# Own buffers and an earlier load for two row chunks of an up projection, and a decode order squeezed by three half features

## The chip, the cores and the metric

The kernel runs on one core of a Trainium2 chip. The metric is the device time of one execution in microseconds (us), the median of three runs. TensorE (PE) multiplies matrices, VectorE (DVE), ScalarE (ACT) and GpSimd (POOL) work on rows of 128 partitions, SyncE (SP) issues most of the DMAs. Every engine has one instruction stream of its own, which it works through in order.

## The reference

One layer step of a hybrid decoder: a 2048-token prompt and eight sample tokens that attend to 4096 cached positions in pages. All arithmetic is float32. The part that matters here is the gated convolutional feed-forward network of the prompt rows, and the paged attention of the samples, which the kernel works on during it:

```python
def conv_ffn(h, prefix, w_up, conv_w, conv_b, w_down):
    up = h @ w_up                                  # h 2064 x 1024, w_up 1024 x 5632
    ...
    c = conv_b + sum(conv_w[i] * ext[:, i:i + L] for i in range(CONV_W))   # CONV_W = 3
    gate, val = c[..., :D_FF], c[..., D_FF:]       # D_FF = 2816 = 22 x 128
    out = (jax.nn.silu(gate) * val) @ w_down
```

For the samples, keys and values (8 heads of 64) are read through `page_table`; the weights come from `sigmoid(q.k)` and a running product of `1 - sigmoid` over later positions.

## The kernel before

Three parts follow each other on PE: the projections, attention and output projection of the prompt, to about 1163 us; the **up projection**, from 1184 to 2263 us; and the **down projection** to the end.

**Up projection.** The normalised rows `h2_s` (in device memory) are cut into four chunks of 512 rows. A chunk's rows are loaded, transposed on PE (tile `tp3c` or `tp0`, four 128x128 transposes into one PSUM buffer) and split into a high part (a cast on ACT, L163) and a low part (a subtraction on DVE, L164); both stand in `h2c[ch]`. Only three chunks have room: chunk 0 in pool `pha`, chunks 1 and 2 in `phb`, and chunk 3 takes chunk 0's place. The main loop runs over 44 features `it`: 0 to 21 take the 22 gate and value blocks of the weights for chunks 0 and 1, 22 to 43 the same blocks for chunks 2 and 3. A feature holds two chunks `k`, each a **pair** of **groups** `s` (gate and value); a group is 24 matmuls (`mm3`: 8 blocks of 128 rows, three products of high and low parts) into one PSUM buffer `psu`. So there are 88 pairs (called steps below) and 176 groups, numbered from 0. Per group, ACT scales the result into `cv` (L976), DVE adds the two convolution taps (L979) and, except for chunk 0, the tile's edge from `carry` (L982, L984), and then copies the last two columns into `carry` (L986). That copy is the last reader of the group's PSUM buffer. The pool `psm` has six such buffers, used in turn by `psu` and by the transposes `tp3c`. The next feature's weights `uwr` are loaded by SP (L703) and split by ACT and DVE (`uwh`, `uwl`).

**Chunks 2 and 3** go through `h2_chunk(ch)`, called at feature 4 for chunk 2 and behind feature 21 for chunk 3. It makes two loads of 256 rows (1 MB, L766) into buffers of the tag `kvd`, and per load 16 transposes (L773) and four splits.

**Decode.** The `kvd` buffers (`KVB` = 4, 1 MB each) are otherwise for the gathers of cached keys and values (`gather`, L813, an indirect DMA that POOL issues; 128 of them). Keys are multiplied and summed on DVE (L826, L828), values multiplied on PE (tile `dav`, L896), all in a written order of 101 items: keys, weights, values, and last the sums. `DSTEP(i)` is the number of items that stand ahead of step i; an item, once placed, calls the gather of a tile three further on. At the last feature (`it` = 43) the remaining items are placed, the decode pool is closed, and the first activations and weights of the down projection are loaded (`act_first`, `wd_first`).

The scheduler orders each engine's stream from the program order and the dependences, so the place of a call in the source doesn't fix its place on an engine.

Of the kernel before, what the change touches and what calls it, by code (L numbers as in the profile page):

```python
# [8 lines left out]
F32 = mybir.dt.float32  # L9
F32R = mybir.dt.float32r  # L10
# [8 lines left out]
P = 128  # L19
D = 1024  # L20
NK = D // P
# [9 lines left out]
NF = DFF // P  # L31
# [6 lines left out]
TILES = [(0, NS + META)] + [(NS + META + P * i, P) for i in range(SEQ // P)]  # L38
# [5 lines left out]
HKB, KFB, CHB = 11, 4, 2  # L44
RAWB = 4
FSTEP = lambda i: 3 * i // 2
DSTEP = lambda i: 101 * i // 85
CW = 512
NCH = SEQ // CW
NSB = NS + 4  # L50
# [4 lines left out]
def f32(ap):  # L55
    return ap.bitcast(F32)
# [3 lines left out]
def hymba_kernel(  # L60
# [7 lines left out]
    nc = tc.nc  # L68
# [24 lines left out]
    h2_s = dram.tile([ACOLS, D], F32, name="h2_s")  # L93
# [6 lines left out]
    ident = con.tile([P, P], F32, name="ident")  # L100
# [61 lines left out]
    def split(hi, lo, src):  # L162
        nc.scalar.copy(hi, src)  # L163
        nc.vector.tensor_tensor(out=lo, in0=src, in1=f32(hi), op=ALU.subtract)  # L164
# [12 lines left out]
    psm = main.enter_context(tc.tile_pool(name="ps_mm", bufs=2, space=PSUM, reuse_waits="tile"))  # L177
# [520 lines left out]
    pha = h2ctx.enter_context(tc.tile_pool(name="h2a", bufs=1, reuse_waits="tile"))  # L698
    h2c = {}

    def load_up(f):
        wr = puw.tile([P, NK, P], F32, name="uwr")
        nc.sync.dma_start(out=wr, in_=w_up[:, f * P:(f + 1) * P].rearrange("(c p) f -> p c f", p=P))  # L703
        wh = puw.tile([P, NK, P], F32R, name="uwh")
        wl = puw.tile([P, NK, P], F32R, name="uwl")
        split(wh, wl, wr)
        return wh, wl

    def load_down(f, pool):
        wr = puw.tile([P, NK, P], F32, name="uwr").rearrange("p c n -> p (c n)")  # L710
        nc.sync.dma_start(out=wr, in_=w_down[f * P:(f + 1) * P, :])
        if pool is puw:
            wh = puw.tile([P, NK, P], F32R, name="uwh").rearrange("p c n -> p (c n)")
            wl = puw.tile([P, NK, P], F32R, name="uwl").rearrange("p c n -> p (c n)")
        else:
            wt = pool.tile([P, 2, D], F32R, name="wd")
            wh, wl = wt[:, 0, :], wt[:, 1, :]
        split(wh, wl, wr)
        return wh, wl, wr
# [4 lines left out]
    psm = ctx.enter_context(tc.tile_pool(name="pu_mm", bufs=6, space=PSUM, reuse_waits="tile"))  # L724
    HF = NF // 2

    def load_act(pool, hf, a0, n):
        ar = pool.tile([P, HF, P], F32, name="ar", bufs=1)
        nc.sync.dma_start(out=ar[:, :, :n], in_=act_s[hf * HF:(hf + 1) * HF, :, a0:a0 + n].rearrange("f p n -> p f n"))
        ah = pool.tile([P, HF, P], F32R, name="ah", bufs=1)  # L730
        al = pool.tile([P, HF, P], F32R, name="al", bufs=1)
        split(ah[:, :, :n], al[:, :, :n], ar[:, :, :n])
        return ah, al

    with ExitStack() as es:
        phb = es.enter_context(tc.tile_pool(name="h2b", bufs=2, reuse_waits="tile"))
# [20 lines left out]
        dec = es.enter_context(ExitStack())  # L757
        dp = dec.enter_context(tc.tile_pool(name="dec", bufs=KVB, reuse_waits="tile"))

        def h2_chunk(ch):  # L760

            h2c[ch] = (pha if ch == 3 else phb).tile([P, 2, NK, CW], F32R, name="h2c")
            for a2 in range(0, 4, 2):
                c0 = TILES[1 + 4 * ch + a2][0]
                xn2 = dp.tile([P, 4, 512], F32, name="xn3", tag="kvd").rearrange("p k f -> p (k f)")
                nc.sync.dma_start(out=xn2.rearrange("p (a d) -> p a d", a=2),  # L766
                                  in_=h2_s[c0:c0 + 2 * P, :].rearrange("(a p) d -> p a d", p=P))
                for a in (a2, a2 + 1):
                    xn = xn2[:, (a - a2) * D:(a - a2 + 1) * D]
                    for c4 in range(0, NK, 4):  # L770
                        tp = psm.tile([P, 4, P], F32, name="tp3c", tag="psu")
                        for c in range(4):
                            nc.tensor.transpose(tp[:, c, :], xn[:, (c4 + c) * P:(c4 + c + 1) * P], ident)  # L773
                        split(h2c[ch][:, 0, c4:c4 + 4, a * P:(a + 1) * P], h2c[ch][:, 1, c4:c4 + 4, a * P:(a + 1) * P], tp)

        def sample_conv():
            sc_v = state_conv.rearrange("b j f -> (b j) f")
# [20 lines left out]
        for b in range(NB):  # L798
            nc.sync.dma_start(out=pt4[:, b:b + 1],
                              in_=page_table[b, :].rearrange("(n o) -> n o", o=1).unsqueeze(1).broadcast_to([NPAGE, 4, 1]))  # L800
# [8 lines left out]
        def gather(t):  # L809

            b, j = divmod(t % 64, 8)
            kvt[t] = dp.tile([P, 4, 512], F32, name="kvd", tag="kvd")
            nc.gpsimd.indirect_dma_start(out=kvt[t].rearrange("p k f -> p (k f)"), out_offset=None,  # L813
                                         in_=ckr if t < 64 else cvr,
                                         in_offset=bass.IndirectOffsetOnAxis(ap=idx[:, b, j:j + 1], axis=0))
# [115 lines left out]
        tiles = []  # L931
        for t in order:
            tiles += [t] if not isinstance(t, tuple) else [t[1], t[1] + 1] if t[0] == "v" else []
        ahead = KVB - 1
        done = [0, ahead]
        for t in tiles[:ahead]:
            gather(t)

        def decode_to(n):
            while done[0] < min(n, len(order)):  # L940
                t = order[done[0]]
                done[0] += 1
                kind, t = t if isinstance(t, tuple) else ("k", t)
                {"k": decode_keys, "v": decode_values, "w": decode_weights}.get(kind, lambda t: decode_sums())(t)
                for _ in range({"k": 1, "v": 2}.get(kind, 0)):
                    if done[1] < 128:
                        gather(tiles[done[1]])
                        done[1] += 1

        ws_next = ws_first  # L950
        for it in range(2 * NF):
            half, f = divmod(it, NF)
            ws = ws_next
            if it + 1 < 2 * NF:
                ws_next = [load_up((it + 1) % NF), load_up(NF + (it + 1) % NF)]
            else:
                decode_to(len(order))
                dec.close()
                pdx = ctx.enter_context(tc.tile_pool(name="pdx", bufs=1, side="right", reuse_waits="tile"))
                act_first = load_act(pdx, 0, 0, P)  # L960
                wd_first = [load_down(c, puw) for c in range(3)]
            if it == 4:
                h2_chunk(2)
            if it == 12:
                sample_conv()
            for k in (2 * half, 2 * half + 1):
                with tc.issue_after(last_dve):
                    decode_to(DSTEP(2 * it + k % 2))
                cv = []
                for s in range(2):  # L970
                    fi = f + s * NF
                    ps = psm.tile([P, CW], F32, name="psu")
                    w = ws[s]
                    mm3(ps, [(w[0][:, c, :], w[1][:, c, :], h2c[k][:, 0, c, :], h2c[k][:, 1, c, :]) for c in range(NK)])
                    t = pu.tile([P, CW], F32, name=f"cv{s}")
                    nc.scalar.activation(out=t, in_=ps, func=AF.Identity, scale=cpar(2, fi), bias=cpar(3, fi))  # L976
                    for d in (1, 0):
                        o = 2 - d
                        nc.vector.scalar_tensor_tensor(out=t[:, o:], in0=ps[:, 0:CW - o], scalar=cpar(d, fi),  # L979
                                                       in1=t[:, o:], op0=ALU.mult, op1=ALU.add)  # L980
                    if k:
                        nc.vector.scalar_tensor_tensor(out=t[:, 0:1], in0=carry[:, 1:2, fi], scalar=cpar(1, fi),  # L982
                                                       in1=t[:, 0:1], op0=ALU.mult, op1=ALU.add)
                        nc.vector.scalar_tensor_tensor(out=t[:, 0:2], in0=carry[:, :, fi], scalar=cpar(0, fi),  # L984
                                                       in1=t[:, 0:2], op0=ALU.mult, op1=ALU.add)
                    last_dve = nc.vector.tensor_copy(carry[:, :, fi], ps[:, CW - 2:CW]).ins  # L986
                    cv.append(t)
                sg = pu.tile([P, CW], F32, name="sg")
                nc.scalar.activation(out=sg, in_=cv[0], func=AF.Sigmoid)
                nc.gpsimd.tensor_tensor(out=cv[1], in0=cv[0], in1=cv[1], op=ALU.mult)  # L990
                nc.gpsimd.tensor_tensor(out=sg, in0=sg, in1=cv[1], op=ALU.mult)
                nc.sync.dma_start(out=act_s[f, :, CW * k:CW * (k + 1)], in_=sg)
            if it == NF - 1:
                h2_chunk(3)

    h2ctx.close()

# [1 line left out]
    with ExitStack() as es:  # L999
# [129 lines left out]
        for hf in range(2):  # L1129
            wd = []  # L1130
            for c in range(HF):
                f = hf * HF + c
# [49 lines left out]
```

## Time and profile before

| | us |
|---|---|
| median of three runs | 2816.26 (2814.99 to 2817.17) |
| the profiled execution | 2817.6, its span 2815.9 |
| PE busy | 2699.1 (96% of the span) |
| DVE busy | 1800.5 (64%) |
| ACT busy | 1041.7 (37%) |
| POOL busy | 837.1 (30%) |

The span is the time from the first to the last instruction that the profiler saw; the rest of the execution's time, 1.7 us, lies around it. Shares are means over the three parts, which differ much.

### The profile page before, as it was taken

How to read it: one execution, taken by the hardware profiler on the slowest of the kernel's cores; microseconds unless marked ns; L12 is line 12 of the kernel's file. 1: busy time of each engine (PE TensorE's matmuls, PEld its weight loads, DVE VectorE, ACT ScalarE, POOL GpSimd, SP SyncE). 2: the span in 40 equal slices, each digit the busy share in tenths (PEclk: the TensorE clock that was granted, in tenths of full speed). 3: DMA queues.
4: the chain of work that ended last, by engine and by line, in shares of the span. 5: the costliest groups of instructions: out<-in, count | busy, mean ns of one | idle time of the engine just before them, and what ended most of it. 6: DMA issues, size and time to landing. Idle time of an engine off the chain costs nothing.

```text
span 2815.9 us, 39585 instructions
## 1 busy us (share of the span) xinstructions
PE 2699.1 (96%) x14623; PEld 2102.5 (75%) x14623; DVE 1800.5 (64%) x2989; ACT 1041.7 (37%) x1817; POOL 837.1 (30%) x995
## 2 busy tenths in 40 slices
PE   5899999999998999897999999999999999999998
PEld 4677777777776887686877777777777767777777
DVE  4587668867678578687977676777765441214434
ACT  4466557656565356422222223222222220002111
POOL 0132233332224023154555544445543200000000
PEclk9899999999998999998999999999999999999999
DMA  7642542454435432554565656546565584666551
GB/s 257 235 160 101 169 171 96 136 203 154 159 95 167 145 103 95 183 186 159 179 224 199 221 187 229 189 176 222 205 218 181 181 298 157 193 204 225 182 176 63
DMA packets 321190, 498.77 MB, mean 177 GB/s; under 512 B 24279, under 2 KB 229351, under 8 KB 304597
## 3 DMA queue, kind: packets, MB, share of 16 engines
q1 hardware_dynamic: 302565, 362.02, 39.1%
q0 software_dynamic: 18432, 134.23, 12.6%
q8 instruction: 115, 1.88, 0.3%
q14 instruction: 78, 0.64, 0.1%
HBM read 395.99 MB, written 100.59 MB: 176 GB/s over the span
## 4 chain that ended last, share of the span: by engine, by line
PE 84%; DVE 6%; DMA 4%; issue 3%; ACT 2%; POOL 1%; SPq 0%; POOLq 0%; DVEq 0%; ACTq 0%
PE psu L169 11%; PE psu L170 11%; PE psu L171 11%; PE psd L169 6%; PE psd L171 6%; PE psd L170 6%; PE po L569 5%; PE psm L169 4%; PE psm L170 4%; PE z L509 4%; PE psm L171 4%; PE tt L554 3%; DVE om L517 2%; PE dav L896 2%; PE pso L171 2%
## 5 line engine op out<-in xcount | busy, mean ns | idle before, releaser
L169 PE MATMUL psu<-h2c,uwh 128*128 128x512 f32 x1408 | 553.9, 393 | 0.0
L170 PE MATMUL psu<-h2c,uwh 128*128 128x512 f32 x1408 | 551.6, 392 | 0.0
L171 PE MATMUL psu<-h2c,uwl 128*128 128x512 f32 x1408 | 550.1, 391 | 0.0
L517 DVE TENSOR_TENSOR_SCAN om<-om,zero 128x513 f32<-128x513 f32 (+5 forms) x360 | 380.5, 1064 | 106.6 <-ACT om L510 58.9
L979 DVE SCALAR_TENSOR_TENSOR cv<-psu,par,cv 128x511 f32<-128x511 f32 x352 | 261.5, 743 | 162.6 <-ACT cv L976 161.0
L522 POOL TENSOR_TENSOR be<-be,om 128x512 f32<-128x512 f32 (+3 forms) x176 | 189.2, 1075 | 582.7 <-DVE om L517 364.3
L990 POOL TENSOR_TENSOR cv<-cv,cv 128x512 f32<-128x512 f32 x88 | 226.3, 2572 | 386.3 <-DVE cv L984 306.9
L169 PEld LDWEIGHTS psu<-h2c,uwh 128*128 128x128 f32 x1408 | 265.2, 188 | 79.0 <-issue 16.9
L170 PEld LDWEIGHTS psu<-h2c,uwh 128*128 128x128 f32 x1408 | 265.0, 188 | 64.0 <-issue 10.6
L171 PEld LDWEIGHTS psu<-h2c,uwl 128*128 128x128 f32 x1408 | 265.0, 188 | 59.7 <-issue 4.8
L510 ACT ACTIVATE om<-z,nbias 128x512 f32<-128x512 f32 (+5 forms) x360 | 213.6, 595 | 178.7 <-PE z L509 117.4
L976 ACT ACTIVATE cv<-psu,par 128x512 f32<-128x512 f32 x176 | 136.5, 776 | 249.9 <-PE psu L171 249.9
L1149 DVE TENSOR_TENSOR xt<-psd,xt 128x512 f32<-128x512 f32 x64 | 44.1, 691 | 286.4 <-PE psd L171 281.5
L511 ACT ACTIVATE be<-z,bias 128x512 f32<-128x512 f32 (+5 forms) x360 | 212.1, 592 | 2.3 <-DVE bm L527 1.2
L170 PE MATMUL psm<-hk,wh 128*128 128x512 f32 x512 | 208.5, 408 | 3.3 <-DVE hk L218 3.2
L169 PE MATMUL psm<-hk,wh 128*128 128x512 f32 x512 | 206.1, 408 | 3.1 <-ACT hk L217 2.6
L171 PE MATMUL psm<-hk,wl 128*128 128x512 f32 x512 | 206.1, 403 | 1.1 <-DVE wl L164 1.1
L163 ACT CAST uwh<-uwr 128x1024 fp32r<-128x1024 f32 x94 | 98.8, 1055 | 286.7 <-PE psu L170 278.2
L170 PE MATMUL psd<-wd,ah 128*128 128x512 f32 x512 | 200.7, 393 | 3.0 <-DVE wd L164 3.0
L169 PE MATMUL psd<-wd,ah 128*128 128x512 f32 x512 | 202.3, 398 | 0.0
L164 DVE TENSOR_TENSOR uwl<-uwr,uwh 128x1024 fp32r<-128x1024 f32 x94 | 121.3, 1293 | 125.2 <-ACT uwh L163 122.8
L171 PE MATMUL psd<-wd,al 128*128 128x512 f32 x512 | 201.1, 394 | 0.0
(240 smaller groups left out, 4816.7 us busy)
## 6 DMA issues: line engine op xcount, KB each, us to landing
hk<-hs_s SPq DMA_DIRECT2D x96, 512.0 KB
uwr<-in_w_up_dram SPq DMA_DIRECT2D x88, 512.0 KB
act_s<-sg SPq DMA_DIRECT2D x88, 256.0 KB
ar<-act_s SPq DMA_DIRECT2D x32, 704.0 KB
raw<-in_w_up_dram SPq DMA_DIRECT2D x40, 512.0 KB
xt<-in_x_prompt_dram SPq DMA_DIRECT2D x32, 512.0 KB
hs_s<-hk SPq DMA_DIRECT2D x32, 512.0 KB
uwr<-in_w_down_dram SPq DMA_DIRECT2D x22, 512.0 KB
```

Of the source, the lines that this page charges most:

```text
L164: nc.vector.tensor_tensor(out=lo, in0=src, in1=f32(hi), op=ALU.subtract)
L169: nc.tensor.matmul(ps, ah, bh, start=i == 0, stop=False)
L170: nc.tensor.matmul(ps, ah, bl, start=False, stop=False)
L171: nc.tensor.matmul(ps, al, bh, start=False, stop=i == n - 1)
L510: nc.scalar.activation(out=om[:M, e, 0:n], in_=z[:M, :n], func=AF.Sigmoid, scale=-SCALE, bias=nbias[:M, h:h + 1])
L511: nc.scalar.activation(out=be[:M, e, 0:n], in_=z[:M, :n], func=AF.Sigmoid, scale=SCALE, bias=bias[:M, h:h + 1])
L517: nc.vector.tensor_tensor_scan(out=rv, data0=rv, data1=zero[:M, 0:1].broadcast_to([M, n + 1]), initial=1.0 if top else st["prev"][:M, e, 0 ...
L522: (nc.gpsimd if cnt["mul"] % 2 == 0 else nc.vector).tensor_tensor(out=be[:M, e, m0:n], in0=be[:M, e, m0:n], in1=om[:M, e, m0 + 1:n + 1], o ...
L569: mm = nc.tensor.matmul(o, v_, a_, start=top and i < (2 if groups else 1), stop=low and i == len(prods) - 1, skip_group_check=True)
L976: nc.scalar.activation(out=t, in_=ps, func=AF.Identity, scale=cpar(2, fi), bias=cpar(3, fi))
L979: nc.vector.scalar_tensor_tensor(out=t[:, o:], in0=ps[:, 0:CW - o], scalar=cpar(d, fi), in1=t[:, o:], op0=ALU.mult, op1=ALU.add)
L990: nc.gpsimd.tensor_tensor(out=cv[1], in0=cv[0], in1=cv[1], op=ALU.mult)
```

## The change

Chunks 2 and 3 get a tag of their own, `xn3`, with two buffers of 128 rows (512 KB each). `h2_load` loads one tile of 128 rows, `h2_turn` transposes and splits it, and for a chunk's first two tiles loads the tile two further on behind it. The loads of tiles 0 and 1 stand one feature ahead of the turn. Chunk 2 is turned in two halves, at features 4 and 5; chunk 3 whole, behind feature 21. The gathers that are made ahead are called at step 2, the decode items run from step 4 to step 84, and the pool is closed and `act_first` loaded at feature 42.

```diff
-DSTEP = lambda i: 101 * i // 85
+DSTEP = lambda i: 101 * max(i - 3, 0) // 81
...
-        def h2_chunk(ch):
-            h2c[ch] = (pha if ch == 3 else phb).tile([P, 2, NK, CW], F32R, name="h2c")
-            for a2 in range(0, 4, 2):
-                c0 = TILES[1 + 4 * ch + a2][0]
-                xn2 = dp.tile([P, 4, 512], F32, name="xn3", tag="kvd").rearrange("p k f -> p (k f)")
-                nc.sync.dma_start(out=xn2.rearrange("p (a d) -> p a d", a=2), ...
+        h2x = {}
+        def h2_load(ch, a):
+            h2x[ch, a] = dp.tile([P, D], F32, name="xn3", bufs=2)
+            nc.sync.dma_start(out=h2x[ch, a], in_=h2_s[TILES[1 + 4 * ch + a][0]:TILES[1 + 4 * ch + a][0] + P, :])
+        def h2_turn(ch, a):
+            if a == 0:
+                h2c[ch] = (pha if ch == 3 else phb).tile([P, 2, NK, CW], F32R, name="h2c")
+            xn = h2x.pop((ch, a))
+            for c4 in range(0, NK, 4):
...
+                split(h2c[ch][:, 0, c4:c4 + 4, a * P:(a + 1) * P], h2c[ch][:, 1, c4:c4 + 4, a * P:(a + 1) * P], tp)
+            if a < 2:
+                h2_load(ch, a + 2)
...
-            else:
+            if it == 2 * NF - 2:
                 decode_to(len(order))
                 dec.close()
...
                 act_first = load_act(pdx, 0, 0, P)
+            if it == 2 * NF - 1:
                 wd_first = [load_down(c, puw) for c in range(3)]
-            if it == 4:
-                h2_chunk(2)
+            for ch, t0 in ((2, 4), (3, NF)):
+                if it == t0 - 1:
+                    h2_load(ch, 0)
+                    h2_load(ch, 1)
+            if it in (4, 5):
+                h2_turn(2, 2 * it - 8)
+                h2_turn(2, 2 * it - 7)
...
             for k in (2 * half, 2 * half + 1):
+                if 2 * it + k % 2 == 2:
+                    for t in tiles[:ahead]:
+                        gather(t)
...
             if it == NF - 1:
-                h2_chunk(3)
+                for a in range(4):
+                    h2_turn(3, a)
```

What becomes of this on the engines is shown at three places. On SP, around the start of the up projection and through features 0 to 5 (`pt` is the page table, `qb` a sample's query), before:

```order
L744 DMA xn_13105<-h_s 128x1024
L703 DMA uwr<-in_w_up_dram 128x8x128
L799 DMA pt_13128<-in_page_table_dram 128x1x1 x8
L819 DMA qb<-qd_s 128x512 x2
...
L703 DMA uwr<-in_w_up_dram 128x8x128
L766 DMA xn_13811<-h_s 128x2x1024
L703 DMA uwr<-in_w_up_dram 128x8x128
L992 DMA act_s<-sg 128x512
L766 DMA xn_13841<-h_s 128x2x1024
```

and now:

```order
L803 DMA pt_13128<-in_page_table_dram 128x1x1 x8
L823 DMA qb<-qd_s 128x512
L765 DMA xn_13638<-h_s 128x1024
L765 DMA xn_13640<-h_s 128x1024
L823 DMA qb<-qd_s 128x512
...
L703 DMA uwr<-in_w_up_dram 128x8x128
L765 DMA xn_13811<-h_s 128x1024
L765 DMA xn_13827<-h_s 128x1024
L703 DMA uwr<-in_w_up_dram 128x8x128
...
L765 DMA xn_16707<-h_s 128x1024
L765 DMA xn_16709<-h_s 128x1024
```

The loads of chunk 2's tiles 0 and 1 moved up to right behind the page table, four features ahead of their turn; those of tiles 2 and 3 stand behind the first half's turn, and chunk 3's first two behind the second half's.

On PE at chunk 3 (behind feature 21), before:

```order
L171 MATMUL psu<-h2c,uwl 128x512
L896 MATMUL dav<-kvd,zdec 32x512 x4
L773 MATMUL tp3c<-ident,xn_16872 128x128 x16
L773 MATMUL tp3c<-ident,xn_16902 128x128 x16
L169 MATMUL psu<-h2c,uwh 128x512
```

and now:

```order
L171 MATMUL psu<-h2c,uwl 128x512
L775 MATMUL tp3c<-ident,xn_16707 128x128 x8
L775 MATMUL tp3c<-ident,xn_16709 128x128 x8
L900 MATMUL dav<-kvd,zdec 32x512 x8
L775 MATMUL tp3c<-ident,xn_16876 128x128 x8
L775 MATMUL tp3c<-ident,xn_16892 128x128 x8
L169 MATMUL psu<-h2c,uwh 128x512
```

At chunk 2, where PE had the same 16 and 16 transposes in one place (ahead of group 16), it now has 8 and 8 there and 8 and 8 ahead of group 20.

On DVE, at the second of these half turns (`cv_13864`, `cv_13894`, `cv_13933` and `cv_13965` are groups 16 to 19; each carry copy frees the PSUM buffer of the group before it), now:

```order
L164 TENSOR_TENSOR h2c<-tp3c,h2c 128x4x128 x2
L996 COPY carry<-psu 128x2
L830 TENSOR_TENSOR kvd<-kvd,qb 128x2048 x2
L989 SCALAR_TENSOR_TENSOR cv_13864<-psu,par,cv_13864 128x511
L832 TENSOR_REDUCE zdec<-kvd 128x4x8 x2
L989 SCALAR_TENSOR_TENSOR cv_13864<-psu,par,cv_13864 128x510
L996 COPY carry<-psu 128x2
L989 SCALAR_TENSOR_TENSOR cv_13894<-psu,par,cv_13894 128x511
L989 SCALAR_TENSOR_TENSOR cv_13894<-psu,par,cv_13894 128x510
L996 COPY carry<-psu 128x2
L830 TENSOR_TENSOR kvd<-kvd,qb 128x2048
L164 TENSOR_TENSOR uwl<-uwr,uwh 128x1024
```

followed by

```order
L989 SCALAR_TENSOR_TENSOR cv_13933<-psu,par,cv_13933 128x511
L992 SCALAR_TENSOR_TENSOR cv_13933<-carry,par,cv_13933 128x1
L832 TENSOR_REDUCE zdec<-kvd 128x4x8
L989 SCALAR_TENSOR_TENSOR cv_13933<-psu,par,cv_13933 128x510
L994 SCALAR_TENSOR_TENSOR cv_13933<-carry,par,cv_13933 128x2
L164 TENSOR_TENSOR uwl<-uwr,uwh 128x1024
L989 SCALAR_TENSOR_TENSOR cv_13965<-psu,par,cv_13965 128x511
L992 SCALAR_TENSOR_TENSOR cv_13965<-carry,par,cv_13965 128x1
L164 TENSOR_TENSOR h2c<-tp3c,h2c 128x4x128 x3
L996 COPY carry<-psu 128x2
```

Before, all eight `h2c` subtractions of chunk 2 stood in one place, behind the copies of groups 14 and 15 and ahead of group 16's taps. Now three of the second half's stand ahead of the copy of group 18 (the last row), which stands behind the first part of group 19.

On POOL the first four gathers stand where they stood, behind the setup of the decode; the fifth, which stood behind the first pair's product, stands behind the third's, and the later ones follow three pairs later than before at first, in step at the end.

## Rows read from the trace of the kernel before

**Rows 1.** The page: busy time and its share of the span, and the share of each engine in the chain that ended last.

```profile
PE 2699.1 (96%) x14623; PEld 2102.5 (75%) x14623; DVE 1800.5 (64%) x2989; ACT 1041.7 (37%) x1817; POOL 837.1 (30%) x995
...
PE 84%; DVE 6%; DMA 4%; issue 3%; ACT 2%; POOL 1%; SPq 0%; POOLq 0%; DVEq 0%; ACTq 0%
```

**Rows 2.** Stretches of the up projection and after: its length, then busy time and instructions of PE, PEld, DVE, ACT and POOL, the granted TensorE clock (1.00 is the higher of its two levels), the DMA share and GB/s.

```profile
1207.00:1272.00 65.00, 65.00 (x288) 53.81 (x288) 55.86 (x63) 18.34 (x24) 36.80 (x18) 1.00 0.51 181
1272.00:1295.00 23.00, 8.39 (x38) 7.49 (x37) 15.97 (x22) 6.79 (x11) 6.92 (x5) 0.67 0.62 210
1295.00:1715.00 420.00, 420.00 (x1936) 329.36 (x1935) 311.81 (x412) 111.15 (x145) 211.57 (x127) 1.00 0.55 193
1720.00:1731.00 11.00, 7.49 (x46) 6.07 (x45) 8.97 (x14) 6.11 (x10) 5.49 (x4) 0.84 0.92 322
...
2263.00:2311.00 48.00, 40.99 (x170) 28.00 (x169) 25.43 (x40) 15.90 (x16) 2.57 (x2) 0.89 0.85 296
```

**Rows 3.** What PE waited for between 1207 and 2315 us: waiting instruction, what released it, us in total, times, longest.

```profile
PE tp3c L773 <- DMA xn<-h_s: 16.0, 3, 9.7
PE psd L169 <- ACT ah L163: 3.6, 1, 3.6
...
PE tp3c L773 <- DVE h2c L164: 2.1, 1, 2.1
```

**Rows 4.** PE's timeline at chunk 2: start, duration, instruction, and in brackets the idle time before it and what ended it.

```profile
1272.34 0.39 PE L171 MATMUL psu<-h2c,uwl 128*128 128x512 f32 x1
1282.41 3.64 PE L773 MATMUL tp3c<-ident,xn 128*128 128x128 f32 x16 [9.69 <-DMA xn<-h_s]
1290.98 3.65 PE L773 MATMUL tp3c<-ident,xn 128*128 128x128 f32 x16 [4.93 <-DMA xn<-h_s]
1294.28 0.78 PE L169 MATMUL psu<-h2c,uwh 128*128 128x512 f32 x1
...
1296.86 0.40 PE L169 MATMUL psu<-h2c,uwh 128*128 128x512 f32 x1
```

**Rows 5.** SP's timeline there: when the loads of chunk 2 were issued.

```profile
1275.45 0.37 SPq L766 DMA_DIRECT2D xn<-h_s  x1
...
1286.09 0.36 SPq L766 DMA_DIRECT2D xn<-h_s  x1
```

**Rows 6.** DVE's timeline there; a row with no bracket started with nothing idle before it, so that the step from one start to the next is what an instruction costs in a row of them.

```profile
1273.14 2.27 DVE L828 TENSOR_REDUCE zdec<-kvd 128x32 f32<-128x2048 f32 x1
1275.34 0.73 DVE L979 SCALAR_TENSOR_TENSOR cv<-psu,par,cv 128x510 f32<-128x510 f32 x1
1276.00 0.20 DVE L984 SCALAR_TENSOR_TENSOR cv<-carry,par,cv 128x2 f32<-128x2 f32 x1
1276.12 1.21 DVE L164 TENSOR_TENSOR uwl<-uwr,uwh 128x1024 fp32r<-128x1024 f32 x1
1277.26 0.74 DVE L979 SCALAR_TENSOR_TENSOR cv<-psu,par,cv 128x511 f32<-128x511 f32 x1
...
1279.09 2.28 DVE L826 TENSOR_TENSOR kvd<-kvd,qb 128x2048 f32<-128x2048 f32 x1
...
1286.95 1.88 DVE L164 TENSOR_TENSOR h2c<-tp3c,h2c 128x512 fp32r<-128x512 f32 x3
```

**Rows 7.** PE's timeline at chunk 3.

```profile
1719.95 0.39 PE L171 MATMUL psu<-h2c,uwl 128*128 128x512 f32 x1
1720.27 1.13 PE L896 MATMUL dav<-kvd,zdec 128*32 128x512 f32 x8
1722.76 1.94 PE L773 MATMUL tp3c<-ident,xn 128*128 128x128 f32 x16 [1.36 <-DMA xn<-h_s]
1726.84 3.56 PE L773 MATMUL tp3c<-ident,xn 128*128 128x128 f32 x16 [2.15 <-DVE h2c L164]
1730.14 0.49 PE L169 MATMUL psu<-h2c,uwh 128*128 128x512 f32 x1
```

**Rows 8.** SP's timeline there.

```profile
1716.13 0.82 SPq L766 DMA_DIRECT2D xn<-h_s  x1
...
1721.46 0.36 SPq L766 DMA_DIRECT2D xn<-h_s  x1
```

**Rows 9.** The chain that ended last, at the start of the up projection (the load of one 512 KB tile of rows, from issue to landing).

```profile
1175.88 5.98 DMA xn<-h_s
```

**Rows 10.** The chain that ended last, at the end of the up projection, and SP's timeline there.

```profile
2264.22 7.62 DMA ar<-act_s
2271.91 10.13 DMA raw<-wf_s
...
2236.69 0.37 SPq L729 DMA_DIRECT2D ar<-act_s  x1
```

**Rows 11.** Gathers of values late in the up projection: POOL's issues, the products on PE that use them (eight records are one gathered tile), and the spread of times from issue to landing of the last 13.

```profile
2160.36 0.99 POOL L813 DMA_INDIRECT kvd<-in_cache_v_dram,idx  x1 [0.16 <-issue]
2165.12 0.98 POOL L813 DMA_INDIRECT kvd<-in_cache_v_dram,idx  x1 [2.45 <-PE dav L896]
...
2168.74 1.13 PE L896 MATMUL dav<-kvd,zdec 128*32 128x512 f32 x8
2174.10 1.13 PE L896 MATMUL dav<-kvd,zdec 128*32 128x512 f32 x8
...
DMA to landing us min/median/max: 5.2/7.5/9.9
```

More of the change, by code (lines that the diff above doesn't have):

```diff
@@ L758, in hymba_kernel @@
         dp = dec.enter_context(tc.tile_pool(name="dec", bufs=KVB, reuse_waits="tile"))
-        def h2_chunk(ch):
-            h2c[ch] = (pha if ch == 3 else phb).tile([P, 2, NK, CW], F32R, name="h2c")
-            for a2 in range(0, 4, 2):
-                c0 = TILES[1 + 4 * ch + a2][0]
-                xn2 = dp.tile([P, 4, 512], F32, name="xn3", tag="kvd").rearrange("p k f -> p (k f)")
[L766 to L774, printed above, removed]
+        h2x = {}
[7 more added lines that the diff above has]
+            for c4 in range(0, NK, 4):
+                tp = psm.tile([P, 4, P], F32, name="tp3c", tag="psu")
+                for c in range(4):
+                    nc.tensor.transpose(tp[:, c, :], xn[:, (c4 + c) * P:(c4 + c + 1) * P], ident)
+                split(h2c[ch][:, 0, c4:c4 + 4, a * P:(a + 1) * P], h2c[ch][:, 1, c4:c4 + 4, a * P:(a + 1) * P], tp)
+            if a < 2:
+                h2_load(ch, a + 2)
         def sample_conv():
@@ L935, in hymba_kernel @@
         done = [0, ahead]
-        for t in tiles[:ahead]:
-            gather(t)
         def decode_to(n):
```

## The prediction

> **What bounds the kernel now.** First the page: PE is busy 96% of the span and holds 84% of the chain that ended last, DVE 64% and 6% [rows 1]. So time is won only where PE stands still or runs at its lower clock. Second, the stretches of the up projection: in most of it PE has no gap at all, 420.00 us busy of 420.00 at a granted clock of 1.00, and the same in the twelve groups ahead of chunk 2, 288 matmuls in 65.00 us, 5.42 us a group [rows 2]. There are three exceptions: 1272 to 1295 us, where PE is busy 8.39 us of 23.00 at 0.67; 1720 to 1731, 7.49 of 11.00; and the passage to the down projection from 2263, 40.99 of 48.00 [rows 2]. Third, the waits name the causes: 16.0 us are transposes waiting for loads of chunk rows, 2.1 us a transpose waiting for DVE, and the passage waits for something else, the activations' split [rows 3]. The reader is to see that the idle time of these stretches, 14.6, 3.5 and 7.0 us, is all there is, and that the change touches the first two.
>
> **Chunk 2, the large term.** The last matmul of group 15 starts at 1272.34; the next could start 0.23 later, and the next group's does at 1294.28: 21.7 us lost. That group's first six matmuls then take 2.58 us (1294.28 to 1296.86) where six at the full rate take 1.36: 1.2 us more for the clock. Together 22.9 us [rows 4]. The 9.69 and 4.93 us of idle time in it are the loads: the first is issued at 1275.45, right after the key reduction of 1273.14 that frees a shared buffer, and the second at 1286.09, behind the first 16 transposes [rows 4, 5, 6]. Now the first two tiles are loaded at the start of the up projection into buffers that nothing else uses, some 85 us before their turn; the other two are issued when the first half's transposes are done and have four groups, 21.7 us, until theirs. One load of this size took 5.98 us [rows 9]. Neither load can be late by these numbers. What stays are 32 transposes, at the full clock 1.94 us for sixteen [rows 7], 3.9 us. Avoidable: 22.9 - 3.9 = 19.0 us.
>
> **What it adds there: a wait for a PSUM buffer.** Splits and groups share six buffers, in turn. Counting back six, group 20, behind the second half's transposes, gets the buffer of group 18, free at group 18's carry copy, and on DVE that copy now has three of the second half's subtractions ahead of it. I follow DVE from the end of group 15 (time 0), with what an instruction costs in a row of them: a key product or reduction 2.2, `uwl` 1.14, a tap 0.66, an edge 0.12, a subtraction 0.61 [rows 6]. Group 15's copy, behind two taps, two edges and four subtractions (4.0 us, after ACT has scaled the group and cast the transposes), is done at about 6. Two products, two reductions and two taps bring group 16's copy to 16.1; two taps group 17's to 17.5; then product, `uwl`, tap, edge, reduction, tap, edge, `uwl`, tap, edge and three subtractions, 10.9 us, group 18's to 28.4. PE needs 1.9 for the first half, 21.7 for four groups, 1.9 for the second half, and wants the buffer at 25.6. So it waits 2.8 us. Ahead of the first half's groups there is no such wait: group 17 takes the buffer of group 15, free at 6, and starts at 7.4. Bounds: nothing, if DVE runs 2.8 us ahead of this count; and 4.5 us, if DVE idles in it as it did before chunk 2, 9.14 of 65.00 us or 14% [rows 2], which over the 12.3 us since group 16's copy is 1.7. I take 2.8. After a wait of this length PE may run at the lower clock for a while: the sixteen transposes behind waits of 1.36 and 2.15 us took 3.56 where the sixteen between those waits had taken 1.94, 1.6 us more [rows 7]. Nothing or 1.6; I take 0.8.
>
> **Chunk 3.** Before, from 1720.18 to 1730.14, 9.96 us, of which 1.13 is a value product that stood there anyway [rows 7]; its loads were issued at 1716.13 and 1721.46 [rows 8]. Now tiles 0 and 1 lie ready, their transposes take 1.94, but tiles 2 and 3 use the same two buffers and can be issued only when these are done, at 1.0 and 1.9. With 0.3 for the issue and 5.98 to land [rows 9], tile 2 is there at 7.3, turned by 8.3, tile 3 by 9.3; the two value tiles now queued between (2.3 us) lie inside the wait. Gain 0.7 us. Before, the 1 MB loads took 4.9 to 7.0 us (1286.09 to 1290.98, 1275.45 to 1282.41) [rows 4, 5], which gives a gain of 1.7 or a loss of 0.4; with the lower clock on the last sixteen a loss of 2, and 3 if DVE doesn't hold the last splits as it did for 2.15 us. I use the 5.98 us, the one row for a load of this size beside other traffic. A rule of the Trainium skill speaks against the smaller loads: "DMA: Bandwidth & Descriptors", section "Bandwidth", wants at least 1 MiB a transfer. Its section "Anatomy of one DMA" gives 2.0 us plus the bytes at 436 GB/s, by which, as an estimate, a 512 KB load takes 3.2 us and a 1 MB load 4.4, and chunk 3 would gain some 3 us, the sum 2798. The trace doesn't agree on the size: 5.98 us for the small load [rows 9].
>
> **The rest, at nothing.** The decode items are 1.247 a step instead of 1.188. Their DVE work, 5% more per step, lies under PE's matmuls: DVE was busy 311.81 of 420.00 us there [rows 2]. If that cover were gone, a key item costs 4.4 us and about one in twenty steps has one more. The first four gathers stand where they did. The activations' first load goes out a feature half earlier, but it was out at 2236.69 and what ends the passage are a later `ar` of 7.62 us and the `raw` behind it, 10.13 us, both issued when the up projection ends [rows 10]; nothing is gained, with 2 us either way for how they share the queues. On SP nothing but weights stands behind the new loads: those behind the half turns wait for PE, and the weights queued behind them are wanted a feature later.
>
> **Sum.** 19.0 - 2.8 - 0.8 + 0.7 = 16.1 us less than the profiled execution, 2817.6, which is 1.3 us above the median: 2816.3 - 16.1 = 2800.2 us.
>
> **The rivals.** (a) *The new waits take more*: 4.5 us for the PSUM buffer and 1.6 for the clock after it, chunk 3 loses 2, the passage 2; gain 19.0 - 10.1 = 8.9, 2807.4 us. For it speaks that DVE does sixteen subtractions in each chunk, which it used to do while PE stood still (15.97 us busy in 23.00), now under PE's groups, where it had only 14% to spare [rows 2]; against it, that six buffers cover some 20 us of lateness.
> (b) *No new wait*: DVE is 3 us ahead, chunk 3 gains 1.7; 20.7 us, 2795.6. The idle 14% speaks against it.
> (c) *The change doesn't do what it says*: SP holds the loads of tiles 2 and 3 behind another wait until the second half's turn, and PE stands there for a load of 6 us and for the PSUM wait, with the same again at chunk 3; 19.0 - 2.8 - 1.6 - 6 - 5 = 3.6, 2812.7, no difference that can be measured. It needs 15 us of lateness on SP; I see nothing of that size.
> (d) *Slower: values come late*. Near the end PE multiplies gathered values 8.4 and 9.0 us after their gathers were issued, and landing took 5.2 to 9.9 us with a median of 7.5 [rows 11]. PE works in order, so a late gather stops it. The items now follow each other 5% closer, which takes about 0.4 us from each such margin. If the last 13 tiles each came late by the 9.9 us less 8.0, 1.9 us, that were 24.7 us, net 8.6 slower: 2824.9. It turns the sign from 1.2 us a tile. Against it: the median still leaves 0.5 us, and before not one wait of PE for a gather appears [rows 3].
>
> **How the numbers follow.** What a measurement here can tell from no change is about 0.2%, 5.6 us. Chances: as summed 0.60, (a) 0.17, (b) 0.13, (c) 0.06, (d) 0.04. The likeliest gives 2800.2, with its own bounds 2796 to 2804. From (b) to beyond (a), 2792 to 2809, leaves out (c), (d) and the tails of (a), under 2 in 10. Faster by over 0.2%, below 2810.6: the sum, (b) and nearly all of (a), 0.88; the same: (c) and a tail of (a), 0.08; slower: (d), 0.04.
>
> **What would show it.** Right: no transposes of chunk 2 waiting for a load; 16 transposes of about 1.94 us ahead of group 16 and of group 20; one wait of 2 to 4 us at group 20, ended by DVE's carry copy of group 18; at chunk 3 a wait of 4 to 5 us for a load of rows between the first and the last sixteen; the passage as before. Wrong: waits of PE for a DMA of `h_s` at chunk 2, PSUM waits in several groups behind group 20, or waits of the value products for gathers.

## The result, and the profile after

The changed kernel takes 2797.45 us (median of four runs, 2794.48 to 2800.8) against 2816.72 for the kernel before: a ratio of 0.9939, 95% interval 0.9927 to 0.9952. Repeated on another chip it took 2799.91 against 2813.82, a ratio of 0.9949, interval 0.9935 to 0.9962. So the change is worth 14 to 19 us; 16.1 were forecast. The profiled execution took 2796.7 us.

The page (answers [rows 1]):

```profile
PE 2688.3 (96%) x14623; PEld 2096.0 (75%) x14623; DVE 1805.8 (65%) x2989; ACT 1039.9 (37%) x1817; POOL 833.3 (30%) x995
```

The stretches (answers [rows 2], with the same columns: us, busy time and instructions of PE, PEld, DVE, ACT and POOL, granted clock, DMA share, GB/s):

```profile
1201.00:1266.00 65.00, 65.00 (x288) 53.83 (x287) 44.87 (x62) 18.51 (x24) 29.27 (x16) 1.00 0.40 134
1266.00:1298.00 32.00, 27.09 (x134) 22.70 (x133) 30.60 (x35) 12.05 (x19) 12.83 (x7) 0.97 0.62 219
1698.00:1709.00 11.00, 7.83 (x53) 5.89 (x52) 9.54 (x14) 6.26 (x11) 6.37 (x4) 0.86 1.03 372
2242.00:2290.00 48.00, 41.05 (x169) 28.53 (x168) 23.77 (x38) 15.62 (x16) 2.57 (x2) 0.86 0.84 289
```

The second stretch is what has become of chunk 2: PE is now busy 27 of 32 us, and DVE 30.60 of 32. The engine that was beside the path now has no slack there. Chunk 3's stretch and the passage are nearly what they were.

What PE waits for in the up projection (answers [rows 3]):

```profile
PE psu L169 <- DVE h2c L164: 4.9, 1, 4.9
PE tp3c L775 <- DVE carry L996: 2.6, 1, 2.6
PE tp3c L775 <- DMA xn<-h_s: 0.6, 1, 0.6
```

The two long waits for loads of chunk 2 are gone. In their place stands one new wait of 4.9 us that DVE ends. PE's timeline at chunk 2 (answers [rows 4]):

```profile
1266.32 1.91 PE L775 MATMUL tp3c<-ident,xn 128*128 128x128 f32 x16
1267.98 0.48 PE L169 MATMUL psu<-h2c,uwh 128*128 128x512 f32 x1
...
1289.87 1.91 PE L775 MATMUL tp3c<-ident,xn 128*128 128x128 f32 x16
1296.68 0.79 PE L169 MATMUL psu<-h2c,uwh 128*128 128x512 f32 x1 [4.91 <-DVE h2c L164]
1297.28 0.63 PE L170 MATMUL psu<-h2c,uwh 128*128 128x512 f32 x1
...
1299.41 0.53 PE L169 MATMUL psu<-h2c,uwh 128*128 128x512 f32 x1
```

The first half turn costs its 1.7 us and nothing else. Behind the second, PE stands from 1291.77 to 1296.68 and then runs six matmuls in 2.73 us. The same stretch on DVE (answers [rows 6]):

```profile
1272.48 0.15 DVE L996 COPY carry<-psu 128x2 f32<-128x2 f32 x1
1272.55 5.71 DVE L830 TENSOR_TENSOR kvd<-kvd,qb 128x2048 f32<-128x2048 f32 x2
...
1283.88 0.14 DVE L996 COPY carry<-psu 128x2 f32<-128x2 f32 x1
...
1285.38 0.15 DVE L996 COPY carry<-psu 128x2 f32<-128x2 f32 x1
1285.44 2.28 DVE L830 TENSOR_TENSOR kvd<-kvd,qb 128x2048 f32<-128x2048 f32 x1
1287.64 2.32 DVE L164 TENSOR_TENSOR uwl<-uwr,uwh 128x1024 fp32r<-128x1024 f32 x1
...
1290.55 0.58 DVE L992 SCALAR_TENSOR_TENSOR cv<-carry,par,cv 128x1 f32<-128x1 f32 x1
...
1295.95 1.87 DVE L164 TENSOR_TENSOR h2c<-tp3c,h2c 128x512 fp32r<-128x512 f32 x3
1297.75 0.14 DVE L996 COPY carry<-psu 128x2 f32<-128x2 f32 x1
```

The copies are those of groups 15, 16, 17 and 18. PE starts group 20 at 1296.68, before the last of them: what it waited for is the first of the three subtractions, done 0.6 us into the row of 1295.95.

Chunk 3 on PE (answers [rows 7]):

```profile
1698.41 1.91 PE L775 MATMUL tp3c<-ident,xn 128*128 128x128 f32 x16
1700.25 1.98 PE L900 MATMUL dav<-kvd,zdec 128*32 128x512 f32 x16
1704.82 1.06 PE L775 MATMUL tp3c<-ident,xn 128*128 128x128 f32 x8 [2.60 <-DVE carry L996]
1706.46 1.94 PE L775 MATMUL tp3c<-ident,xn 128*128 128x128 f32 x8 [0.57 <-DMA xn<-h_s]
1708.06 0.78 PE L169 MATMUL psu<-h2c,uwh 128*128 128x512 f32 x1
```

and on SP (answers [rows 8]), where both loads of the second half were issued together:

```profile
1699.48 1.19 SPq L765 DMA_DIRECT2D xn<-h_s  x2
```

From the end of group 87 to the start of group 88 it still takes 9.65 us, where it took 9.96, and of that 2.0 are now value products, where 1.1 were.

### The profile page after: what moved, and what is told of

Same layout as the page of the kernel before. It is cut to its first block, busy times and chain, and to the rows that moved or that the text cites. A ratio compares the mean times of both kernels' runs of the same rounds, so it can differ in the third digit from the quotient of the medians.

```text
span 2795.0 us, 39581 instructions
## 1 busy us (share of the span) xinstructions
PE 2688.3 (96%) x14623; PEld 2096.0 (75%) x14623; DVE 1805.8 (65%) x2989; ACT 1039.9 (37%) x1817; POOL 833.3 (30%) x995
## 4 chain that ended last, share of the span: by engine, by line
PE 86%; DVE 5%; DMA 3%; issue 3%; ACT 2%; POOL 1%; SPq 0%; POOLq 0%; DVEq 0%; ACTq 0%
PE psu L169 11%; PE psu L170 11%; PE psu L171 11%; PE psd L169 6%; PE psd L171 6%; PE psd L170 6%; PE po L569 5%; PE psm L169 4%; PE psm L170 4%; PE psm L171 4%; PE z L509 4%; PE tt L554 3%; PE dav L900 2%; DVE om L517 2%; PE pso L169 2%
## 5 line engine op out<-in xcount | busy, mean ns | idle before, releaser
L1000 POOL TENSOR_TENSOR cv<-cv,cv 128x512 f32<-128x512 f32 x88 | 219.0, 2489 | 366.2 <-DVE cv L994 289.4
L554 PE MATMUL tt<-ident,be 128*128 128x128 f32 x1088 | 168.7, 280 | 20.7 <-POOL om L504 5.9
```

The source lines that it names most:

```text
L554: nc.tensor.transpose(tt[:, a, e, :M], be[:M, e, lo_:lo_ + P], ident[:M, :M])
```

## The experiments

Single times scatter by several us (the kernel before: 2811.18 to 2819.76 in nine runs on one chip), so the runs are compared by two numbers: the median with its ratio to the kernel before on the same chip, and, from each profile, the length of the **up projection**, from the first matmul of group 0 to the end of group 175, which repeats to within 2.5 us.

```
                                       median    ratio to before (95%)    start of up   its length
before, three profiles                 2813-2818                          1183.6 1178.9 1184.2   1079.6 1079.4 1081.0
changed kernel, two profiles           2797.45   0.9939 (0.9927-0.9952)   1179.2        1062.9
                          again        2799.91   0.9949 (0.9935-0.9962)   1180.4        1065.2
own buffers alone                      2796.44   0.9934 (0.9918-0.9951)   1180.9        1064.5
decode order alone                     2802.07   0.9953 (0.9937-0.9970)   1179.0        1072.2
chunk 2 turned at features 1 and 2     2792.05   0.9918 (0.9902-0.9935)   1181.3        1058.6
chunk 3's second half at group 90      2795.06   0.9926 (0.9909-0.9942)   1183.2        1060.1
both of these                          2789.78   0.9916 (0.9902-0.9929)   1180.1        1054.1
chunk 2 one tile a feature, and the
  second half of chunk 3 at group 90   2788.41   0.9904 (0.9889-0.9919)   1182.6        1053.5
```

**Is part of the gain ahead of the change?** The profile after starts the up projection 4.4 us earlier than that of before (1179.2 against 1183.6), in a part that the change doesn't touch. The kernel before was profiled twice more.

> The kernel before, profiled once more. The profile of before reached the first group of the up projection at 1183.6 us, the profiles of ten runs of changed kernels at 1179.0 to 1183.2, and the decode half alone gained 12.2 us by its times but only 7.4 between the first and the last group of the up projection. Theory (what lies ahead of the up projection scatters by some 4 us from execution to execution, and the change does nothing there): this profile starts the up projection between 1179 and 1184 us and takes 1079 to 1080 us for it again. Rival (something in the changed programs shortens the part ahead): 1183 us or later.

> The kernel before a third time, for the same question: by scatter the up projection starts between 1179 and 1184 us and takes 1079 to 1080; by the rival it starts at 1183 us or later again.

First matmul of group 0, first and second of the two:

```profile
1178.93 0.78 PE L169 MATMUL psu<-h2c,uwh 128*128 128x512 f32 x1
```

```profile
1184.17 0.78 PE L169 MATMUL psu<-h2c,uwh 128*128 128x512 f32 x1
```

Both ends of the range, for the same program: scatter. (The expectation speaks of ten profiles of changed kernels; the record has nine, which start between 1179.0 and 1183.2 us.) The length of the stage repeated (1079.4 and, one above what was expected, 1081.0). By that length the change is worth 1080.0 less 1064.0, 16 us.

**One half of the change, own buffers alone.** The edit, on the changed kernel:

```diff
-DSTEP = lambda i: 101 * max(i - 3, 0) // 81
+DSTEP = lambda i: 101 * i // 85
...
-            if it == 2 * NF - 2:
+            else:
                 decode_to(len(order))
                 dec.close()
```

and the first gathers called ahead of the loop again.

> The change's own buffers, early loads and half turns alone; the decode items, the first gathers and the closing of the pool as in the kernel before. Theory (the gain is chunk 2's loads out of PE's way, the decode squeeze is worth nothing by itself): no wait of PE for a load of chunk 2, 2797 us plus or minus 4. Without the double decode item between the half turns (10 us of DVE work in a row becomes 4.4) the 4.9 us wait at group 20 goes; but DVE comes to the first half turn with a double item behind it, so a wait of about 4 us for a PSUM buffer should stand at group 16 instead. Rival (part of the gain comes from the squeezed decode, its earlier end and the earlier load of the activations): 2803 us or more. Second question: the profile after the change reached the first group of the up projection 4.4 us earlier than that of before, in a part that the change doesn't touch. If that is scatter between executions, this run's start may lie anywhere between 1179 and 1184 us.

The time came out as expected, and so did the place of the wait. PE at the first half turn:

```profile
1269.84 1.91 PE L775 MATMUL tp3c<-ident,xn 128*128 128x128 f32 x16
1276.06 0.50 PE L169 MATMUL psu<-h2c,uwh 128*128 128x512 f32 x1 [4.31 <-DVE h2c L164]
```

A wait of 4.3 us ahead of group 16, none ahead of group 20. So the own buffers alone do as much as the whole change (up projection 1064.5 us against 1062.9 and 1065.2). They turn a wait for loads into a smaller wait for DVE, and where that stands depends on which step holds a double decode item (two items in one step: two products and two reductions on DVE).

**The other half, the decode order alone**, on the kernel before:

```diff
-DSTEP = lambda i: 101 * i // 85
+DSTEP = lambda i: 101 * max(i - 3, 0) // 81
...
+                if 2 * it + k % 2 == 2:
+                    for t in tiles[:ahead]:
+                        gather(t)
```

and the pool closed at feature 42.

> The other half alone: the decode items from step 4 to 84, gathers called at step 2, the pool closed at feature 42; chunks 2 and 3 loaded as in the kernel before, through the shared buffers. Theory: PE's wait for chunk 2's loads is back, 14 to 15 us of it, and the time is 2816 us plus or minus 4. Rival: 2810 us or less, if the squeeze brings a part of the gain.

This expectation fell: 12.2 us by the medians, 7.8 by the length of the up projection. SP and then PE at chunk 2:

```profile
1264.95 0.38 SPq L766 DMA_DIRECT2D xn<-h_s  x1
...
1274.84 0.37 SPq L766 DMA_DIRECT2D xn<-h_s  x1
```

```profile
1271.37 3.44 PE L773 MATMUL tp3c<-ident,xn 128*128 128x128 f32 x16 [3.25 <-DMA xn<-h_s]
1280.07 3.64 PE L773 MATMUL tp3c<-ident,xn 128*128 128x128 f32 x16 [5.26 <-DMA xn<-h_s]
```

The wait for the first load is 3.25 us instead of 9.69 [rows 4]. With the decode three steps behind, the shared buffer that the load needs was free before group 15 ended, and the load was issued 3.2 us ahead of that end, while PE still had work; before, it was issued 2.9 us behind it. Both halves of the change thus attack the same standstill: 15.5 us (by length) for the buffers, 7.8 for the order, 16 together. That the order is worth nothing holds only beside the own buffers. By the medians the order alone gained some 4 us more than by its length. Its profile has an early start (1179.0); where its other runs started isn't known, and the interval, 8.4 to 17.7 us, has room for the difference. It was not followed further.

**Is it decode work on DVE that makes group 20 wait?** Chunk 2 turned at features 1 and 2, when no decode item has begun:

```diff
-            for ch, t0 in ((2, 4), (3, NF)):
+            for ch, t0 in ((2, 1), (3, NF)):
...
-            if it in (4, 5):
-                h2_turn(2, 2 * it - 8)
-                h2_turn(2, 2 * it - 7)
+            if it in (1, 2):
+                h2_turn(2, 2 * it - 2)
+                h2_turn(2, 2 * it - 1)
```

> The changed kernel with chunk 2 turned at features 1 and 2 (loads called at feature 0), when no decode item runs on DVE yet. Theory A (the 4.9 us wait at group 20 and the 1.5 us of lower clock behind it come from DVE being late, two decode items ahead of the splits): no PSUM wait at either half turn, 6 us less than the changed kernel, 2791 us. Theory B (a half turn takes four of the six PSUM buffers and the group behind it has to wait for the splits in any case): a wait of 2 us or more stands at group 8 too and the time is 2795 to 2799 us. Theory C (loads this early collide with the first weights): PE waits for uwr or for rows in features 0 to 2, 2800 us or more.

Theory A held. The same turns, and no wait at either:

```profile
1204.90 1.91 PE L775 MATMUL tp3c<-ident,xn 128*128 128x128 f32 x16
1206.56 0.48 PE L169 MATMUL psu<-h2c,uwh 128*128 128x512 f32 x1
```

```profile
1228.42 1.91 PE L775 MATMUL tp3c<-ident,xn 128*128 128x128 f32 x16
1230.09 0.48 PE L169 MATMUL psu<-h2c,uwh 128*128 128x512 f32 x1
```

The up projection takes 1058.6 us, 5.4 less than the changed kernel's mean of 1064.0. Theory C fell with it: PE waited for no load there.

**What made DVE later than counted?** Some DVE rows under the new wait are longer than [rows 6] gave for their like: a weights' subtraction of 2.32 us where 1.21 was usual, an edge of 0.58 for 0.20. In this run GpSimd's two products of feature 4 are left out (`if it != 4:` ahead of both).

> The changed kernel with the two products of GpSimd left out at feature 4 (four instructions on groups 16 to 19; their results are missing from the output). In the changed kernel the low-part subtraction of the weights behind group 17's copy took 2.3 us on DVE where others take 1.2, and an edge 0.58 where others take 0.2, at the time when GpSimd multiplies. Theory (the two engines slow each other): these rows fall to 1.2 and 0.2, group 18's copy comes 1.5 us sooner, and the wait at group 20 is 3.0 to 3.7 us instead of 4.9. Rival (the subtraction waits for something else): the rows stay as they are, and so does the wait.

DVE and then PE, at the same place in the program:

```profile
1292.51 1.22 DVE L164 TENSOR_TENSOR uwl<-uwr,uwh 128x1024 fp32r<-128x1024 f32 x1
...
1294.31 0.21 DVE L992 SCALAR_TENSOR_TENSOR cv<-carry,par,cv 128x1 f32<-128x1 f32 x1
```

```profile
1300.08 0.80 PE L169 MATMUL psu<-h2c,uwh 128*128 128x512 f32 x1 [3.44 <-DVE h2c L164]
1300.67 0.63 PE L170 MATMUL psu<-h2c,uwh 128*128 128x512 f32 x1
...
1305.36 0.59 PE L169 MATMUL psu<-h2c,uwh 128*128 128x512 f32 x1
1305.79 0.40 PE L170 MATMUL psu<-h2c,uwh 128*128 128x512 f32 x1
```

The rows fall to 1.22 and 0.21, and the wait to 3.4 us: GpSimd's products do slow these DVE rows. That DVE slows GpSimd in turn no run tests; in the changed kernel GpSimd's product at that time took 3.27 us, where it took 1.30 some 14 us earlier (the mean of its 88 is 2.49):

```profile
1271.51 1.30 POOL L1000 TENSOR_TENSOR cv<-cv,cv 128x512 f32<-128x512 f32 x1 [6.73 <-DVE cv L994]
...
1285.61 3.27 POOL L1000 TENSOR_TENSOR cv<-cv,cv 128x512 f32<-128x512 f32 x1 [1.10 <-ACT uwh L163]
```

The Trainium skill has the rule for it: "SBUF — State Buffer", section "Who interferes with whom", says that a DVE instruction with two inputs in SBUF contends with a GpSimd instruction that reads SBUF. The weights' subtraction is such an instruction, and the runs agree: 2.32 us beside GpSimd, 1.22 without. But no time was gained (1066.1 us for the up projection): PE's wait was 1.5 us shorter, and the stretch at the lower clock behind it (a granted clock of 0.50 in both kernels) twelve matmuls long (1300.08 to 1305.36) instead of six. Group 20 took 8.3 us where it took 7.0 in the changed kernel and 5.4 is usual. This is one profile; whether a shorter wait brings a longer slow stretch isn't shown.

**Where is chunk 3's time?** Its second half turned ahead of group 90, the first that reads chunk 3:

```diff
             if it == NF - 1:
-                for a in range(4):
-                    h2_turn(3, a)
+                h2_turn(3, 0)
+                h2_turn(3, 1)
...
+                if it == NF and k == 3:
+                    h2_turn(3, 2)
+                    h2_turn(3, 3)
```

> The changed kernel with the second half of chunk 3 (tiles 2 and 3, which are loaded again into the same two buffers) turned ahead of group 90, the first one that reads chunk 3, instead of ahead of group 88. At chunk 3 the changed kernel loses 9.4 us from group 87's end to group 88's start, of which 3.9 are transposes. Theory (what stands there is the reload and a PSUM buffer that DVE frees late): groups 88 and 89 cover both, the waits of 2.6 and 0.6 us go, and the value products no longer stand in a gap but still cost their 2 us: 3 to 5 us less than the changed kernel, 2793 to 2794 us. Rival (PE waits for the same DVE work two groups later): 2797 us, with a PSUM wait ahead of group 90.

PE ahead of group 88 and ahead of group 90:

```profile
1703.86 1.91 PE L775 MATMUL tp3c<-ident,xn 128*128 128x128 f32 x16
1705.70 1.98 PE L900 MATMUL dav<-kvd,zdec 128*32 128x512 f32 x16
1707.61 0.50 PE L169 MATMUL psu<-h2c,uwh 128*128 128x512 f32 x1
...
1718.65 1.91 PE L775 MATMUL tp3c<-ident,xn 128*128 128x128 f32 x16
1720.49 1.12 PE L900 MATMUL dav<-kvd,zdec 128*32 128x512 f32 x8
```

No wait is left at chunk 3; the one at group 20 stays (4.9 us). The up projection is 3.9 us shorter than the changed kernel's mean; the medians, 2795.06 against 2797.45 and 2799.91, are too close to tell by themselves.

**Do the two add?** Both edits together, beside the changed kernel once more, and a version that turns chunk 2 one tile a feature:

> The changed kernel once more, beside the others of this call. The two halves of the change gave 17.9 and 12.2 us each, alone, and 19.3 together, so they don't add. Theory: both shorten the same standstill at chunk 2 (the own buffers take the loads out of the queue for decode buffers; the squeezed decode frees a shared buffer 8 us sooner), and the whole change gains what the own buffers gain, less the wait of 4.9 us at group 20 that the squeeze moved there from group 16 (4.3): 16 to 18 us below the kernel before on the same chip. The first group of the up projection starts anywhere from 1179 to 1184 us, and what is ahead of it moves the time of single runs by some 4 us.

> The changed kernel with both edits that helped: chunk 2 turned at features 1 and 2, before the decode begins, and the second half of chunk 3 turned ahead of group 90. Theory: the two savings lie at different places and add, 6 us (the wait at group 20 and the clock behind it) and 4 us (the waits between the halves of chunk 3): 9 to 11 us below the changed kernel in the same call. Rival (the work that DVE is spared at one place is late at the next): no more than 6 us.

```diff
-            if it in (4, 5):
-                h2_turn(2, 2 * it - 8)
-                h2_turn(2, 2 * it - 7)
+            if 4 <= it < 8:
+                h2_turn(2, it - 4)
```

> The changed kernel with chunk 2 turned one tile a feature, at features 4 to 7, under the running decode, and the second half of chunk 3 ahead of group 90. A turn then takes two of the six PSUM buffers at a time and adds four subtractions less to DVE's queue. Theory A (it is DVE's backlog of decode items that makes the group behind a turn wait): the waits shrink to 0 to 2 us and the time is within 2 us of the kernel that turns chunk 2 before the decode. Theory B (each turn costs a wait of its own): four waits of 2 to 4 us, slower than the kernel that only moves chunk 3's second half.

They add: 2789.78 us, 10.1 below the changed kernel on the same chip, and 9.9 by the length of the stage. One tile a feature does as well under the running decode, 2788.41 us, and its intervals (0.9889 to 0.9919, and 0.9935 to 0.9962 for the changed kernel) don't touch. PE's timeline of it at the first and the second of the four turns:

```profile
1271.06 1.03 PE L775 MATMUL tp3c<-ident,xn 128*128 128x128 f32 x8
1271.85 0.47 PE L169 MATMUL psu<-h2c,uwh 128*128 128x512 f32 x1
...
1293.74 1.03 PE L775 MATMUL tp3c<-ident,xn 128*128 128x128 f32 x8
1294.53 0.48 PE L169 MATMUL psu<-h2c,uwh 128*128 128x512 f32 x1
```

In neither version does PE wait for anything within the up projection. With one tile a feature DVE still had a double item between the first two turns (two products, 5.58 us, at 1276.21), and with the own buffers alone four PSUM buffers went to the second half turn, behind single items, without a wait. So it isn't the decode work alone, nor the splits alone, that made group 20 wait: it takes four PSUM buffers given to one turn and a double decode item on DVE together. Which of the two versions is better can't be told.

## Why the prediction was right

The time lies 2.7 us from the forecast, and by the length of the up projection the change is worth 16 us against 16.1. That is closer than the terms were, and in part luck. In the first pair of profiles the terms below come to 19.2 - 4.9 - 1.5 + 1.9 = 14.7 us. The rest of that pair's 16.7 us (1079.6 less 1062.9) lies ahead of chunk 2, nearly all of it in group 0: 7.4 us before, 5.6 after. In the repeat group 0 took 7.1 us, and in the other profiles of the kernel before 7.3 and 6.8, so this part isn't the change's.

- **Loads out of the way, 19.0 us.** Right in mechanism and size: no transposes of chunk 2 wait for a load, and the sixteen take 1.91 us. Groups 12 to 20 take 59.1 us where they took 71.9, 12.8 less; with the new wait (4.9) and the slow group behind it (1.5) added, the loads gave 19.2.
- **The wait for a PSUM buffer, 2.8 us.** The step that was mis-sized, twice. The place, group 20, and the engine were right. The buffer was not: counting back six says group 18's, but PE went on when the first subtraction of the same turn was done, so it held the buffer of the turn's first transposes. In all three waits of this kind (group 20; group 16 with the buffers alone; chunk 3's third tile, released by group 87's copy at 1704.57 us) the buffer is the next one that DVE frees in its own order. That it is handed out by that order is inferred from these three. The right buffer would have given a shorter wait, 1.6 us by the same count (28.4 less the copy and two subtractions behind it, 27.2, against 25.6). The other error went the other way: DVE reached that subtraction 30.2 us after group 15 instead of 27.2, since product pairs took 5.63 us for two instead of 4.4 (1.2), the weights' subtraction 2.24 (1.1) and an edge 0.50 (0.4) beside GpSimd. (For the products that cause is argued: with GpSimd's products of feature 4 left out the pair still took 5.70 us, beside one of feature 3.) [rows 6] shows the short rows, and I took those; just ahead of them the trace of the kernel before held the long ones too:

```profile
1269.75 2.31 DVE L164 TENSOR_TENSOR uwl<-uwr,uwh 128x1024 fp32r<-128x1024 f32 x1
...
1272.64 0.58 DVE L982 SCALAR_TENSOR_TENSOR cv<-carry,par,cv 128x1 f32<-128x1 f32 x1
```

- **The clock behind it, 0.8 us.** It was 1.5 in the changed kernel (group 20 took 6.95 us where 5.44 is usual) and 1.7 in the repeat, about the upper bound of 1.6, and 2.8 in the run with the shorter wait.
- **Chunk 3, 0.7 us.** From group 24 on the stage is 1.9 us shorter, nearly all of it at chunk 3: 0.3 is the stretch itself, and 1.4 a second tile of value products that now lies inside it. The forecast saw that tile there but didn't count that it is gone from between other groups. The loads were on time within the estimate: issued together from 1699.48 us on, the second was there when PE went on at 1706.46, some 6 us after its issue. (The 3.2 us that the prediction estimated from the Trainium skill, "DMA: Bandwidth & Descriptors", section "Anatomy of one DMA", was not reached; that section's fit is for DMAs issued by GpSimd, and SP issues these. The 2798 us that went with it lies nearer the result still, but not for its reason.) But the third tile waited for DVE (2.60 us), not for its load as forecast; in the repeat it was the load (2.94): both end at nearly the same time.
- **The decode order, nothing.** Right beside the own buffers, and wrong as a statement on the order by itself: the alone run shows that it frees a shared buffer sooner. The cover that I named, DVE's idle share, was the right thing to ask for, but at the wrong place: it is gone for 30 us around the half turns.
- **The passage, nothing.** Right: 543.4 us from the end of the up projection to PE's last matmul, 543.1 before; over all profiles it lies between 541 and 544.

Of the rivals, (a) is what happened at group 20: its first two terms, 6.1 us in sum, were 6.4, with chunk 3 and the passage not losing as it had them. Its sixteen subtractions in each chunk are a slip: there are eight, one for every four transposes. (c) did not come: SP issued the loads of tiles 2 and 3 from 1267.38 us on, 22 us ahead of their transposes. (d), late values, did not come: the gather with the least room was issued 7.7 us ahead of its use, landing took up to 11.8 us, and still no wait for one appears in PE's list, since those that landed late were wanted later.

## What to carry to other kernels

When a load is taken off the path, ask what the waiting engine hid: here DVE did a chunk's eight subtractions while PE stood still, and had to find room for them under full work afterwards. A burst that takes most of a small pool's buffers is best cut to pieces of two buffers, or put where the engine that frees them is idle: with chunk 3's second half moved too, that brought another 10 us beside the change's 16. Two edits that shorten the same wait don't add, so measure each alone before crediting it.

## What the runs showed of the hardware

The price of a wait on PE is not its length alone: a wait of 4.91 us was followed by six matmuls at the lower clock (granted clock 0.50), one of 3.44 us at the same place, in a single profile, by twelve, and the sums differ by 0.2 us. And a DVE subtraction of two SBUF operands took 2.32 us beside a GpSimd product, 1.22 without; the product beside it took 3.27 us, where one 14 us earlier took 1.30.
